# Sink logits from one bfloat16 product of three parts, and a shorter 1/sqrt, in a two-layer transformer kernel

## The chip, the core and the metric

The kernel runs on one core of one Trainium2 chip. The metric is the device time of one execution in microseconds. Differences are told in per cent of the time before, 2735.24 us.

## The reference, cut to what matters

The program is a trunk of two layers over 512 latent tokens and 256 context tokens with 1024 features. Each layer is a SwiGLU feed-forward, a mixer and a second feed-forward, every one behind an RMS norm with modulation. The mixer of layer 0 has two groups of heads, latent attention and window attention; that of layer 1 is gated linear attention. The window attention gives every query one more logit, the sink of its head, which takes part in the softmax and has no value:

```python
s_win = jnp.where(valid, s_win, NEG_INF)
s_ctx = jnp.einsum("bqngd,bknd->bngqk", qi, kc) * WIN_SCALE
pr = jax.nn.softmax(jnp.concatenate([s_ctx, s_win, sink_col], axis=-1), axis=-1)
```

The sink is one number for each of the 8 heads, the same for all queries. RMS norms stand in front of each sub-layer, on the queries and keys of both kinds of attention, on the latents, and on the outputs of the gated linear attention:

```python
rms_norm(t, g) = t / sqrt(mean(t * t) + 1e-6) * g
```

## The kernel before, in words

All large products are made of float32 data in three passes: a matrix is split into a high and a low part of type float32r (ScalarE copies the high part at L127, VectorE subtracts at L128), and TensorE multiplies high by high, high by low and low by high (L356 to L358, L368). TensorE takes its instructions in order; a weight load (PEld) and a product (PE) belong to each of them.

The layer-0 mixer is `pair_mixer`. Its first instructions (load of the norm gains at L722 and L724, the two scalings at L726 and L727, a bfloat16 identity at L729, the load of the sinks at L732, and the first weights) are issued while the last products of the feed-forward before it still run. The sinks lie in one row as [1, 8, 2] float32: the logit of each head, and beside it -1e30, so that a product has two columns.

Window attention runs in two calls of `win_attention`, one for each key/value head with its four query heads. `run_units` goes over 20 units in each: 4 units of context queries with two heads each, and 16 of latent queries with one head, which makes 24 score rows in a call and 48 in both. For one score row (`scores`, L1121 to L1137) TensorE multiplies the queries with the 256 context keys, with the window's keys, adds the band mask by a bfloat16 product with the identity (L1130; latent queries alone), and writes the sink into the two columns behind the scores:

```python
one = self.ones[0:1, :]
nc.tensor.matmul(out=s[:, n:n + 2], lhsT=one, rhs=sink[:, 4 * c + hd, :], start=True, stop=True)
```

The second line is L1137. Operands of plain float32 are multiplied in two passes, so it leaves two weight loads and two products in the trace. VectorE then takes the maximum of the row (L1065, tile nm), ScalarE the exponential (L1070), VectorE the reciprocal of the sum (L1032), GpSimd the scaling (L1035), TensorE transposes (L712), ScalarE and VectorE split the result (L1059, L1074), and TensorE multiplies with the values (L1158). Under it, in equal shares for every unit, other work of the mixer runs: in the first call the remaining input projections and the norm of the queries, in the second `latents`, with its keys, values and queries (tiles kn, va, qa), up to the norm of the first latent queries.

`rsqrt` (L130 to L144) gives 1/sqrt on small tiles, of 2 to 48 columns: a shift (L137) and a subtraction (L139) for a first guess, then three rounds of three operations (L142, L143, L144), all on VectorE, each needing the one before it. It is called 23 times: once at the start, in the norm ahead of the later sub-layers (tile rstd), eight times inside the layer-0 mixer (tile rs), and once for each of the 4 heads of the gated linear attention (tile gr).

The order of the instructions in each engine's queue is not that of the code alone. The program is built under `tile.TileContext(nc, schedule_with_timeline_sim=True)`: a planner follows its own estimate of all durations and, among the instructions that it takes to be ready, issues those first that stand earlier in the code or under `high_priority`.

Of the kernel before, what the change touches and what calls it, by code (L numbers as in the profile page):

```python
# [8 lines left out]
F32 = mybir.dt.float32  # L9
# [13 lines left out]
T = SEQ + CTX  # L23
# [4 lines left out]
ALL_SEGS = [(0, 256), (256, 512), (512, T)]  # context tokens, latent tokens  # L28
# [3 lines left out]
class Stage:  # L32
    """A sub-layer: loads its first weights, one unit after the other, then waits for its operand."""
# [14 lines left out]
class Net:  # L48
# [28 lines left out]
    # ---- the residual: four slots that hold other things inside a mixer, while it waits in DRAM --  # L77
# [25 lines left out]
    def load_split(self, src, n, pool=None, keep=4, slots=(None, None)):  # L103
        """n columns in two halves, each as (hi, lo)"""
        nc = self.nc
        res = []
        for j in range(2):
            raw = self.raw(src[:, j * (n // 2):(j + 1) * (n // 2)])
            p, bufs = (self.stage, 3) if pool is None else (pool, keep)
            if slots[j]:  # L110
                hi, lo = [self.x_slot(i, [128, n // 2], F32R) for i in slots[j]]
            else:
                hi = p.tile([128, 1024], F32R, tag="whi", name="whi", bufs=bufs)[:, :n // 2]
                lo = p.tile([128, 1024], F32R, tag="wlo", name="wlo", bufs=bufs)[:, :n // 2]
            self.split(raw, hi, lo)
            res.append((hi, lo))
        return res
# [7 lines left out]
    def split(self, src, hi, lo, e=None):  # L125
        """src (float32, SBUF) -> hi + lo, both float32r"""
# [4 lines left out]
    def rsqrt(self, out, v, shape):  # L131
        """out = 1/sqrt(v) for a small positive float32 tile"""
# [3 lines left out]
        t = self.small.tile(shape, F32, tag="rs_t", name="rs_t", bufs=1)  # L136
        nc.vector.tensor_scalar(out=i, in0=v.bitcast(I32), scalar1=1, scalar2=None,  # L137
# [3 lines left out]
        for _ in range(3):  # L141
            nc.vector.tensor_tensor(out=t, in0=out, in1=out, op=ALU.mult)  # L142
            nc.vector.scalar_tensor_tensor(out=f, in0=t, scalar=-0.5, in1=v, op0=ALU.mult, op1=ALU.mult)  # L143
            nc.vector.scalar_tensor_tensor(out=out, in0=f, scalar=1.5, in1=out, op0=ALU.add, op1=ALU.mult)  # L144

# [20 lines left out]
    def mod_finish(self, l, p):  # L166
        """bias; the scale piece becomes norm_g * (1 + scale), the FFN gates carry the 1/2"""
# [11 lines left out]
    def first_open(self, pool):  # L179
        """silu(c), silu(c_ctx) and zeros; the sum of four groups of 32 rows"""  # L180
# [14 lines left out]
    def first_product(self, pool, raw):  # L195
        """256 features of the vectors on the tensor engine, four products of 32 columns side by side"""
# [13 lines left out]
    def first_norm(self, pool, m, raw):  # L210
        """shift and scale of the first sub-layer, 128 features"""
# [7 lines left out]
    def first_gate(self, pool, i, raw):  # L219
        """half of the gate of the first sub-layer, 256 features"""  # L220
# [5 lines left out]
    def first_stats(self, pool):  # L226
        """1/rms of all tokens, on every partition"""
# [27 lines left out]
    def mod_queue(self, *pieces):  # L255
        """the products of the pieces (layer, number), in the two halves of the sums"""
# [6 lines left out]
    def mod_half(self, i):  # L263
        """a half of silu(c) and of silu(c_ctx) on every partition, for the background products"""
# [35 lines left out]
    def norm_squares(self, pool, seg, order=range(KT)):  # L300
        """sum over the features of a partition of the squares"""
# [13 lines left out]
    def norm_stats(self, seg, acc):  # L315
        """1/rms of each token of the segment, on every partition (PSUM)"""
# [36 lines left out]
    def mm3(self, out, w, x, first, last):  # L353
        """out += w^T x, w = (hi, lo) stationary, x = (hi, lo) moving"""
# [5 lines left out]
    def pair(self, w, nk, xk, segs, outs, cols=(0, 1)):  # L360
        """two column tiles of a weight unit, w[j] = (hi, lo) of [128, nk * 128], against the
        feature-major operand xk[k] = (hi, lo); outs[seg][j] are PSUM regions"""
# [9 lines left out]
    def regions(self, segs):  # L372
        """PSUM for two column tiles of each segment"""
# [22 lines left out]
    def close_out(self, load, nk, xk, segs, gate, nxt, off=0):  # L396
        """The last products of a sub-layer, in two passes over the weights: the norm of the first tokens runs
        under the products of the others, theirs under the first products of the next sub-layer, whose first
        weights come ahead of all that."""
# [46 lines left out]
    def ffn(self, l, sub, idx, segs, nxt, bg=(0, 0), first=4, start=False):  # L446
# [3 lines left out]
        # the first tiles: without the last segment, under the norm of it  # L450
# [9 lines left out]
        with st:  # L460
# [7 lines left out]
            def up(f, ss, regs=None):  # L468
                """the hidden tile f for the segments ss"""
# [13 lines left out]
            if start:  # L483
                # as the features come
# [61 lines left out]
    def seven_open(self, st, h, n0):  # L546
        """Gate and up columns (rows 1, 2) of a hidden tile against halves of the features and of the tokens,
        in seven products of halves in place of eight (Winograd's form of Strassen's)."""
# [50 lines left out]
        def start():  # L599
            """the place of the fourth block is free now"""  # L600
# [57 lines left out]
    def bcast(self, ap, n):  # L658
        """[128, a, b] -> [128, a, b, n] with a stride of zero"""
        return ap.unsqueeze(len(ap.shape)).to_broadcast(list(ap.shape) + [n])  # L660

    def rms_scale(self, pool, groups, shape, pool_squares=False):
        """1/rms of each group: groups = list of (ap [128, t, g, d], slice of the stats tile)"""
# [21 lines left out]
    def rope(self, pool, out, x, tab, nh, half):  # L685
        """x, out [128, nh, 2 * half] of one token tile; tab = (cos * gain, sin * gain) [128, 2 * half]"""
# [12 lines left out]
    def rot_tables(self, pool, nm, cos, sin, gain, d):  # L699
        """cos * gain and sin * gain, [128, 4, d]"""  # L700
# [14 lines left out]
    def pair_mixer(self, nxt, l=0):  # L715
        """Window attention of the first key/value head runs between the rest of the input projections,
        that of the second between the products of the latent attention's heads."""
        nc, tc, ins = self.nc, self.tc, self.ins
        with ExitStack() as es:
# [5 lines left out]
            # the score scales go with the query gains  # L725
# [5 lines left out]
            sink = ms.tile([1, 8, 2], F32, name="sink")  # L731
            nc.sync.dma_start(out=sink, in_=ins["sink_row"])  # L732
# [4 lines left out]
            z2 = wq[:, :, 4:8, :]  # window keys and values, until the second query chunk  # L737

            # window keys and the first queries: all but the last tokens under the norm of those
# [7 lines left out]
            def product(a, w, n, t, ks):  # L747
                """token tile t of a column chunk, token-major"""
# [56 lines left out]
            zk = self.x_slot(0, [128, 6, 192])  # latent keys, rotary keys, zeros  # L805
# [12 lines left out]
            oT = [None, None] + [self.x_slot(i, [128, 2, T]) for i in (2, 3)]  # MLA, window  # L818
# [8 lines left out]
            def background(gen, share):  # L827
                """a part of the work for each unit of attention; gen yields what it has spent"""
# [42 lines left out]
    def mixer_out(self, name, oT, segs, gate, nxt, oh=()):  # L871
        """oh: what is already in parts"""
# [12 lines left out]
    def norm_rope(self, pool, z, ng, parts):  # L885
        """the first ng groups of z [128, 6, .., 64] in place: RMS norm; then the gain and, for latent tokens, the
        rotation of each part (first group, last, gain, tables)"""
# [25 lines left out]
    def latents(self, lp, ml, zk, zq, gain, gcol, tabs, qa, kn, va, kr, kb):  # L913
        """MLA: normalised latents -> queries, keys, values, token-major"""
# [27 lines left out]
        def put(lat, w, out, sl, n):  # L942
            """token tiles of w^T lat for half of the columns"""
# [35 lines left out]
    def latent_queries(self, lp, gain, tabq, qa, t0):  # L979
        """norm and rotation of the MLA queries of two token tiles"""  # L980
# [15 lines left out]
    def rotary_keys(self, ml, kr, kb):  # L996
        nc = self.nc
        # rotary keys, shared by the heads: rows 64..95 of both key buffers
# [21 lines left out]
    def run_units(self, sp, units, score, probs, values, lanes):  # L1020
        """Attention, one unit after the other, every engine in this order: the scores of unit i, the
        transposition of the probabilities of unit i - 2, the products with the values that ended with
        unit i - 3; ahead of those, the other work of this iteration. A unit is one tile of queries of a
        head or two that see the context only; score(u) gives (PSUM scores, columns, key tiles) of each."""
# [53 lines left out]
    def win_attention(self, wp, c, wq, kT, vs, sink, identb, band, oT, bg):  # L1078
        """the four heads of key/value head c"""
        nc = self.nc  # L1080
        one = self.ones[0:1, :]
# [186 lines left out]
    def split_scaled(self, ps, col, hi, lo):  # L1268
        """PSUM * column -> hi + lo"""
# [6 lines left out]
    def gla_mixer(self, nxt, l=1):  # L1276
        """Both directions of a head run together, between the projections of the next head; the decays of
        the next head are ready before its keys and queries, which meet them on the way out of PSUM."""
# [8 lines left out]
        with ExitStack() as es:  # L1287
# [6 lines left out]
            # rows: high parts, low parts, high parts; those of the other factor: high, high, low  # L1294
# [524 lines left out]
```

## Time and profile before

| | |
|---|---|
| time, median of 3 runs | 2735.24 us (2733.0 to 2736.42) |
| span of the profiled execution, first to last instruction | 2731.1 us |
| TensorE products, busy | 2639.5 us (97%), 16848 instructions |
| TensorE weight loads, busy | 2450.8 us (90%), 16848 instructions |
| VectorE, busy | 2171.2 us (80%), 4540 instructions |
| ScalarE, busy | 1197.9 us (44%) |
| GpSimd, busy | 170.3 us (6%) |
| mean granted TensorE clock | 0.987 |

The profiled execution has no time of its own beside its span; the median of the runs is 4.1 us above that span. Times inside the execution are counted from its first instruction. [...]

### The profile page before, as it was taken

How to read it: one execution, taken by the hardware profiler on the slowest of the kernel's cores; microseconds unless marked ns; L12 is line 12 of the kernel's file. 1: busy time of each engine (PE TensorE's matmuls, PEld its weight loads, DVE VectorE, ACT ScalarE, POOL GpSimd, SP SyncE). 2: the span in 40 equal slices, each digit the busy share in tenths (PEclk: the TensorE clock that was granted, in tenths of full speed). 3: DMA queues.
4: the chain of work that ended last, by engine and by line, in shares of the span. 5: the costliest groups of instructions: out<-in, count | busy, mean ns of one | idle time of the engine just before them, and what ended most of it. 6: DMA issues, size and time to landing. Idle time of an engine off the chain costs nothing. (4 is left out here: it accounts for less than half of the span.)

```text
span 2731.1 us, 44146 instructions
## 1 busy us (share of the span) xinstructions
PE 2639.5 (97%) x16848; PEld 2450.8 (90%) x16848; DVE 2171.2 (80%) x4540; ACT 1197.9 (44%) x2254; POOL 170.3 (6%) x206
## 2 busy tenths in 40 slices
PE   7999999999978899999999999999999999899999
PEld 5899999989867789999999899999998999899899
DVE  5689798977788877797989877978777677778677
ACT  4324242445656753333324542424244555534444
POOL 0000000013344300000000000000000121000000
PEclk9999999999989999999999999999999999999999
DMA  8143444431000050433433314343233112422234
GB/s 311 41 144 119 137 132 143 132 126 31 24 24 1 1 170 24 126 120 122 130 124 110 126 47 144 100 149 105 91 105 102 55 63 70 147 64 97 96 108 130
DMA packets 103461, 279.30 MB, mean 102 GB/s; under 512 B 12146, under 2 KB 15090, under 8 KB 101714
## 3 DMA queue, kind: packets, MB, share of 16 engines
q1 hardware_dynamic: 103250, 276.49, 31.3%
q8 instruction: 132, 2.16, 0.3%
q14 instruction: 79, 0.65, 0.1%
HBM read 269.11 MB, written 7.34 MB: 101 GB/s over the span
## 5 line engine op out<-in xcount | busy, mean ns | idle before, releaser
L127 ACT ACTIVATE whi<-raw 128x512 fp32r<-128x512 f32 (+3 forms) x466 | 356.0, 767 | 730.7 <-PE r L368 324.2
L128 DVE TENSOR_TENSOR wlo<-raw,whi 128x512 fp32r<-128x512 f32 (+3 forms) x466 | 400.1, 861 | 72.3 <-ACT whi L127 69.7
L596 PE MATMUL r<-t,whi 128*128 128x384 f32 (+1 forms) x1704 | 401.2, 323 | 2.8 <-DVE u L633 2.0
L596 PE MATMUL r<-hh,wlo 128*128 128x384 f32 (+1 forms) x1136 | 366.3, 323 | 0.2
L596 PE MATMUL r<-hh,whi 128*128 128x384 f32 (+1 forms) x1136 | 365.8, 322 | 0.0
L596 PE MATMUL r<-hl,whi 128*128 128x384 f32 (+1 forms) x1136 | 365.8, 322 | 0.0
L291 DVE SCALAR_TENSOR_TENSOR junk<-wm,cb 128x512 bf16<-128x512 f32 x480 | 328.8, 685 | 13.1 <-ACT cb L270 8.0
L596 PEld LDWEIGHTS r<-t,whi 128*128 128x128 f32 x1704 | 295.6, 188 | 4.5 <-DVE u L633 2.8
L596 PE MATMUL r<-t,wlo 128*128 128x384 f32 (+1 forms) x852 | 273.3, 323 | 0.2 <-DVE wlo L128 0.2
L368 PE MATMUL r<-dh,whi 128*128 128x512 f32 (+1 forms) x952 | 267.3, 345 | 0.8 <-ACT whi L127 0.8
L368 PE MATMUL r<-dh,wlo 128*128 128x512 f32 (+1 forms) x952 | 266.8, 346 | 0.3 <-DVE wlo L128 0.3
L368 PE MATMUL r<-dl,whi 128*128 128x512 f32 (+1 forms) x952 | 266.8, 344 | 0.0
L127 ACT ACTIVATE whi<-s 128x512 fp32r<-128x512 f32 x284 | 174.9, 625 | 187.5 <-DVE s L618 75.2
L596 PEld LDWEIGHTS r<-hh,wlo 128*128 128x128 f32 x1136 | 213.4, 188 | 1.3 <-DVE wlo L128 1.3
L596 PEld LDWEIGHTS r<-hl,whi 128*128 128x128 f32 x1136 | 213.4, 188 | 0.8
L596 PEld LDWEIGHTS r<-hh,whi 128*128 128x128 f32 x1136 | 213.4, 188 | 0.3
L368 PEld LDWEIGHTS r<-dh,wlo 128*128 128x128 f32 x952 | 178.6, 188 | 24.3 <-DVE wlo L128 1.1
L368 PEld LDWEIGHTS r<-dh,whi 128*128 128x128 f32 x952 | 178.0, 188 | 24.5 <-ACT whi L127 2.7
L368 PEld LDWEIGHTS r<-dl,whi 128*128 128x128 f32 x952 | 178.1, 188 | 23.5
L128 DVE TENSOR_TENSOR wlo<-s,whi 128x512 fp32r<-128x512 f32 x284 | 190.6, 683 | 2.8 <-ACT whi L127 2.1
L392 DVE SCALAR_TENSOR_TENSOR x<-r,mod,x 128x512 f32<-128x512 f32 (+1 forms) x168 | 100.0, 631 | 87.3 <-PE r L368 86.9
L596 PEld LDWEIGHTS r<-t,wlo 128*128 128x128 f32 x852 | 159.9, 188 | 0.5 <-DVE wlo L128 0.5
(403 smaller groups left out, 5880.4 us busy)
## 6 DMA issues: line engine op xcount, KB each, us to landing
raw<-gu SPq DMA_DIRECT2D x176, 512.0 KB, 4.0
wm<-w_mod SPq DMA_DIRECT2D x240, 256.0 KB, 2.9
raw<-dn SPq DMA_DIRECT2D x88, 320.0 KB, 2.9
raw<-dn SPq DMA_DIRECT2D x64, 384.0 KB, 3.1
raw<-w_out SPq DMA_DIRECT2D x28, 512.0 KB, 3.7
m<-w_mod0a SPq DMA_DIRECT2D x12, 1024.0 KB, 10.2
raw<-w_in SPq DMA_DIRECT2D x8, 512.0 KB, 4.5
raw<-w_kq SPq DMA_DIRECT2D x8, 512.0 KB, 3.6
```

Source lines behind the costliest of these rows:

```text
L127: self.nc.scalar.activation(out=hi, in_=src, func=AF.Copy)
L128: (e or self.nc.vector).tensor_tensor(out=lo, in0=src, in1=hi.bitcast(F32), op=ALU.subtract)
L291: nc.vector.scalar_tensor_tensor(out=junk, in0=w, scalar=1.0, in1=self.cb[:, v, :], op0=ALU.mult, op1=ALU.mult, accum_out=self.acc[:, m, v ...
L368: nc.tensor.matmul(out=outs[s][j], lhsT=w[j][wi][:, k * 128:(k + 1) * 128], rhs=xk[k][xi][:, s0:s1], start=(k == 0 and i == 0), stop=(k == ...
L392: self.nc.vector.scalar_tensor_tensor(out=self.xs[m][:, s0:s1], in0=regs[s][j], scalar=gate[:, m, v:v + 1], in1=self.xs[m][:, s0:s1], op0= ...
L596: nc.tensor.matmul(out=o, lhsT=y[wi], rhs=x[k][xi], start=first and k == 0 and i == 0, stop=last and k == H - 1 and i == 2, skip_group_che ...
```

## The change

The sink logits are split once, ahead of the attention, into three bfloat16 parts that add up to the float32 number. The parts lie in rows 0, 32 and 64 of a [96, 8, 2] bfloat16 tile that is zero elsewhere, and one product with 96 rows of ones adds them. The ones are the upper halves of the float32 ones, read with a step of two elements. The loop over parts works in a pool that is closed again before the next tiles are made. In `rsqrt` the three rounds become one round of higher order with four operations and one with three, with other constants: 9 operations in place of 11. The rest of the diff takes comments and docstrings away.

```diff
-            sink = ms.tile([1, 8, 2], F32, name="sink")
-            nc.sync.dma_start(out=sink, in_=ins["sink_row"])
+            sink = ms.tile([96, 8, 2], BF16, name="sink")
+            nc.vector.memset(sink, 0.0)
+            sks = ExitStack()
+            sk = self.pool("sk", sks, side="right")
+            sink_f = sk.tile([96, 8, 2], F32, name="sink_f")
+            nc.sync.dma_start(out=sink_f, in_=ins["sink_row"].to_broadcast([96, 8, 2]))
+            sink_p = sk.tile([96, 8, 2], BF16, name="sink_p")
+            for r in (0, 32, 64):
+                nc.vector.tensor_copy(out=sink_p, in_=sink_f)
+                nc.vector.tensor_copy(out=sink[r:r + 1], in_=sink_p[r:r + 1])
+                if r < 64:
+                    nc.vector.tensor_tensor(out=sink_f, in0=sink_f, in1=sink_p, op=ALU.subtract)
+            sks.close()
...
-        one = self.ones[0:1, :]
+        one = self.ones.bitcast(BF16).rearrange("p (c two) -> p c two", two=2)[0:96, :, 1]
...
-        for _ in range(3):
-            nc.vector.tensor_tensor(out=t, in0=out, in1=out, op=ALU.mult)
-            nc.vector.scalar_tensor_tensor(out=f, in0=t, scalar=-0.5, in1=v, op0=ALU.mult, op1=ALU.mult)
-            nc.vector.scalar_tensor_tensor(out=out, in0=f, scalar=1.5, in1=out, op0=ALU.add, op1=ALU.mult)
+        nc.vector.tensor_tensor(out=t, in0=out, in1=out, op=ALU.mult)
+        nc.vector.tensor_tensor(out=f, in0=t, in1=v, op=ALU.mult)
+        stt(out=t, in0=f, scalar=-10.0 / 3.0, in1=f, op0=ALU.add, op1=ALU.mult)
+        stt(out=out, in0=t, scalar=5.0, in1=out, op0=ALU.add, op1=ALU.mult)
+        stt(out=t, in0=out, scalar=9.0 / 64.0, in1=out, op0=ALU.mult, op1=ALU.mult)
+        stt(out=f, in0=t, scalar=-3.0 / 16.0, in1=v, op0=ALU.mult, op1=ALU.mult)
+        stt(out=out, in0=f, scalar=9.0 / 16.0, in1=out, op0=ALU.add, op1=ALU.mult)
```

## Rows read from the trace of the kernel before

**Rows 1.** Stages of window attention: length, busy PE, PEld, DVE, ACT, POOL (count), clock.
```profile
640.50:656.00 15.50, 15.50 (x105) 14.30 (x104) 5.47 (x15) 8.94 (x25) 5.16 (x10) 0.89 0.01 1
656.00:723.00 67.00, 62.56 (x483) 57.85 (x481) 55.70 (x169) 40.14 (x99) 20.88 (x31) 0.97 0.12 35
723.00:735.00 12.00, 12.00 (x58) 9.99 (x56) 6.24 (x17) 7.51 (x22) 5.00 (x9) 0.72 0.00 0
735.00:759.00 24.00, 22.36 (x145) 18.58 (x143) 21.07 (x60) 19.15 (x46) 12.11 (x17) 1.00 0.06 24
759.00:777.50 18.50, 12.25 (x56) 9.60 (x57) 12.27 (x23) 7.92 (x16) 6.71 (x7) 0.72 0.08 28
777.50:806.50 29.00, 27.30 (x192) 25.18 (x190) 22.70 (x54) 20.76 (x49) 13.85 (x14) 1.00 0.02 2
806.50:836.00 29.50, 18.70 (x76) 14.65 (x76) 28.98 (x82) 9.95 (x25) 15.77 (x16) 0.60 0.11 36
```

**Rows 2.** Sink products, by tile: loads (minimum/median/maximum ns) and who waits.
```profile
L1137 PEld LDWEIGHTS s<-sink,ones x96: 181/184/333, 641.0 to 806.3; 1*128 1x128 f32 x96
...
  DVE nm L1065: 14.2, 14
```

**Rows 3.** Timeline of weight loads around one sink: start, duration, line.
```profile
658.20 0.10 PEld L1130 LDWEIGHTS <-identb 128*128 128x128 bf16 x1
658.36 0.29 PEld L1137 LDWEIGHTS s<-sink,ones 1*128 1x128 f32 x2
658.67 0.20 PEld L712 LDWEIGHTS t<-ident,pr 128*128 128x128 f32 x2
```

**Rows 4.** Timeline of weight loads around a band product with window keys behind it.
```profile
669.32 0.10 PEld L1130 LDWEIGHTS <-identb 128*128 128x128 bf16 x1
669.32 0.31 PEld L1126 LDWEIGHTS s<-wkT,wqT 128*128 128x128 f32 x2
```

**Rows 5.** Timeline in the latent attention: loads of 96 and of 128 rows.
```profile
839.45 0.28 PE L358 MATMUL s<-kb,q 96*128 96x256 f32 x1
839.47 0.25 PEld L712 LDWEIGHTS t<-ident,pr 128*128 128x128 f32 x2
...
845.55 0.38 PE L712 MATMUL t<-ident,qa 128*96 128x128 f32 x2
845.66 0.19 PEld L358 LDWEIGHTS s<-kb,q 96*128 96x128 f32 x1
```

**Rows 6.** An operation of 1/sqrt inside the layer-0 mixer, by tile (minimum/median/maximum ns).
```profile
L143 DVE SCALAR_TENSOR_TENSOR rs_f<-rs_t,ss x24: 157/191/1040, 614.4 to 826.9; 128x32 f32<-128x32 f32 x9, 128x36 f32<-128x36 f32 x3, 128x24 f32<-128x24 f32 x3, 128x12 f32<-128x12 f32 x3
```

**Rows 7.** Timeline at the norm of the latents: GpSimd and TensorE.
```profile
758.87 6.04 POOL L959 TENSOR_TENSOR kn<-kn,rs 128x512 f32<-128x512 f32 x6 [1.83 <-DVE rs_t L142]
...
765.78 1.79 PE L712 MATMUL t<-ident,x 128*128 128x128 f32 x6 [5.91 <-DVE x L965]
```

**Rows 8.** Timeline at the end of the gated linear attention.
```profile
2325.76 0.16 DVE L144 SCALAR_TENSOR_TENSOR gr<-rs_f,gr 128x4 f32<-128x4 f32 x1
2325.96 1.66 DVE L1649 SCALAR_TENSOR_TENSOR sg<-o,gr,sg 128x256 f32<-128x256 f32 x4
2326.50 1.97 PE L712 MATMUL c<-ident,sg 128*128 128x128 f32 x8 [4.56 <-DVE sg L1649]
```

**Rows 9.** Timeline where the mixer's first instructions stand, all engines.
```profile
526.03 0.42 SPq L724 DMA_DIRECT2D gcol<-gain_col  x1
...
526.50 0.33 SPq L732 DMA_DIRECT2D sink<-sink_row  x1
...
529.55 0.15 DVE L727 TENSOR_SCALAR gcol<-gcol 128x1 f32<-128x1 f32 x1 [0.84 <-DMA gcol<-gain_col]
529.62 0.95 DVE L128 TENSOR_TENSOR dl<-sg,dh 128x768 fp32r<-128x768 f32 x1
...
530.62 0.38 PE L368 MATMUL b<-dl,whi 128*128 128x256 f32 x1 [1.16 <-DVE dl L128]
```

**Rows 10.** Busy time and clock in the stretch behind that.
```profile
532.00:540.00 8.00, 8.00 (x57) 7.91 (x56) 6.64 (x17) 4.27 (x8) 0.00 (x0) 0.82 0.49 150
```

More of the change, by code (lines that the diff above doesn't have):

```diff
@@ L136, in rsqrt @@
         t = self.small.tile(shape, F32, tag="rs_t", name="rs_t", bufs=1)
+        stt = nc.vector.scalar_tensor_tensor
         nc.vector.tensor_scalar(out=i, in0=v.bitcast(I32), scalar1=1, scalar2=None,
```

## The prediction

> **What bounds the kernel now.** The busy times of the page come first: TensorE's products fill 97% of the span, so an edit pays where TensorE runs without a break and its own work gets shorter, or where it stands still for exactly the work that is cut. Both parts of the change lie mostly in the window attention of layer 0, so the next view is the table of stages [rows 1]. The reader is to see two kinds of stage in it. From 640.5 to 656 and from 723 to 735 TensorE is busy 15.50 us of 15.50 and 12.00 of 12.00, while VectorE is busy a third to a half and ScalarE about 60%: TensorE alone sets the pace. From 656 to 723, 735 to 759 and 777.5 to 806.5 it is busy 93 to 94%, but VectorE also 78 to 88%, so work taken from TensorE is soon stopped by VectorE. From 806.5 to 836 VectorE is busy 28.98 us of 29.50 and TensorE waits. [...]
>
> The third view is the sink tile [rows 2]: 96 loads, two for each of 48 score rows, and VectorE's maxima waited 14 times, 14.2 us in all, for the sink, because it ends each score row. The fourth is the timeline of loads [rows 3]. Behind the band's load at 658.20 the sink's first load comes 0.16 us later, and the next load only 0.31 us after that, at 658.67, though a sink product has two columns. Where a band product has window keys behind it, the next load starts in the same hundredth as its own, 669.32 [rows 4]. So the sink costs more than two short products: nothing is loaded ahead under it.
>
> **The sink product.** Removed for each score row are two loads and two products of one row; added are one load and one product of 96 rows in bfloat16. What that saves has two parts. The second pass goes in any case: the two loads together take 0.29 us [rows 3], one alone 0.184 [rows 2], so the second begins 0.11 us after the first. The rest is the loading ahead. Loads of 96 rows occur in the latent attention: one starts at 845.66, while products of 128 rows started at 845.55 still run, and a load of 128 rows starts at 839.47, 0.02 us after a product of 96 rows [rows 5]. A change between 96 and 128 rows thus keeps the loading ahead, a change to one row and back does not. If the new sink behaves like the band's bfloat16 load and product [rows 4], its load-to-load distance falls from 0.31 us to about 0.01, and a little of the 0.16 us ahead of it goes too; I take 0.05 of that. That makes 0.35 us for each sink, with 0.11 (the pass alone) and 0.47 (all of 0.31 + 0.16) as ends. A bfloat16 load of 96 rows with a step of two elements stands nowhere in the trace; the band's, with 128 rows and dense, is the nearest.
>
> [...] In the trace the one-row load waits, and loads of 96 and 128 rows run ahead [rows 3, 5]. [...]
>
> How much of 48 x 0.35 = 16.8 us reaches the end follows from the stages, which hold 8, 16, 8, 8 and 8 sinks (no sink from 759 to 777.5 and none behind 806.5). In 640.5 to 656 and 723 to 735 all of it: 8 x 0.35 = 2.8 us each. In 656 to 723, 735 to 759 and 777.5 to 806.5 I take half: 16 x 0.35 / 2 = 2.8, and 1.4 twice, since VectorE has 11.3, 2.9 and 6.3 us free there and its waits are in part for other engines. Sum: 2.8 + 2.8 + 2.8 + 1.4 + 1.4 = 11.2 us.
>
> **1/sqrt.** Each call loses two operations of VectorE. Each depends on the one before and starts 0.20 us behind it (2325.76 to 2325.96, [rows 8]), so 0.4 us a call, 23 calls. Where does TensorE wait for it? At the end of the gated linear attention it stands still for 4.56 us behind that chain [rows 8]: 0.4 us gained in full. At 765.78 it had waited 5.91 us for the norm of the latents [rows 7]. There operations of 1/sqrt on six columns took up to 1040 ns [rows 6], each beside one of GpSimd's six multiplications of 6.04 us in all. Two operations fewer would be worth 2 us if the long ones went; but GpSimd's six stay, as many operations will again be paired with them, and what goes are short ones: 0.4 us. In the VectorE-bound stretch from 797 on lie three calls, six operations of 0.19 us (median, [rows 6]): 1.1 us. Sum 1.9 us. The other 18 calls run under TensorE's products and I cost them at nothing; if their cover were gone, they would give 18 x 0.4 = 7.2 us more. A loss is excluded, since the kinds and sizes of operation remain and there are fewer.
>
> **The new preparation.** Nine operations of VectorE (a clear, six copies, two subtractions) and a load that VectorE must now wait for. Before, the sinks' load concerned only TensorE, over 100 us later. SyncE issues it at 526.50, 0.47 us behind that of gcol, which landed when VectorE went on at 529.55, after 0.84 us of waiting; behind that in VectorE's queue stood the split of dl, and TensorE waited 1.16 us for it [rows 9]. At the same 3.5 us the sinks land near 530.0. [...] Ends 0 and 3.6 us; I take 1.6.
>
> **Sum.** 11.2 + 1.9 - 1.6 = 11.5 us less. Against the profiled span that is 2731.1 to 2719.6 us; the median of the runs is 4.1 us above the span, so 2735.2 - 11.5 = 2723.7, rounded **2724 us**, 0.4% faster. About 0.2% (5.5 us) is what a measurement of this kernel tells from no change, so faster means below 2729.8.
>
> **Rivals.**
> 1. The loading ahead doesn't come: a change to 96 rows, the other type or the step of two still makes the next load wait, as it does behind the one-row product [rows 3]. Then 48 x 0.11 = 5.3 us are saved, two thirds of it (11.2 of 16.8, as above) on the path: 3.5 + 1.9 - 1.6 = 3.8 us, 2731 us. For it: no such load in the trace. Against it: [rows 4, 5].
> 2. VectorE takes over as the bound. If the three mixed stages give nothing, the two pure ones give 5.6 us: 5.6 + 1.9 - 1.6 = 5.9 us, 2729 us. For it: VectorE's 88% from 735 to 759 [rows 1]. Against it: the maxima waited 14.2 us for the sink itself [rows 2].
> [...]
>
> **How the numbers follow.** The forecast has 0.60, rival 1 0.17, rival 2 0.14, rival 3 0.09. The forecast's own range is 2714 to 2730. Its fast end: 0.47 us for each sink with the same shares is 15.0 us, no cost of preparation, some cover gone in the 18 calls (4 us): 15.0 + 1.9 + 4 = 21 us. Its slow end: 11.5 less the rest of the preparation's price (2 us) and half of the mixed stages' 5.6. The range of 8 in 10 reaches to rival 1 with its own 2 us: 2714 to 2733. Faster: 0.58 of the forecast, 0.05 of rival 1, 0.08 of rival 2, so 0.71. Same: 0.02 + 0.12 + 0.06 = 0.20. Slower: 0.09.
>
> **What would show it.** In the changed profile there is one load and one product for each of 48 sinks, and the load behind it starts within 0.05 us rather than 0.31; if it starts 0.1 to 0.2 us later, rival 1 holds. VectorE's wait for sinks falls below 14.2 us. The two pure stages shrink by about 2.8 us each; if they do and the mixed ones don't, rival 2 holds. TensorE's wait for the gate of the gated linear attention falls from 4.56 us to about 4.2. Near 530, the nine operations stand ahead of or behind dl, and TensorE's wait there says what they cost. [...]

## The result, and the profile after

The changed kernel takes 2716.22 us (median of 4 runs, 2714.96 to 2720.14) beside 2734.12 us (4 runs, 2730.45 to 2736.42) for the kernel before: a ratio of 0.9945, 95% interval 0.9930 to 0.9961. It is 17.9 us faster, where 11.5 were forecast. 2716 lies inside the range of 2714 to 2733, near its fast end.

The head of the page after, with the span and TensorE's line:

```profile
span 2715.1 us, 44020 instructions
...
PE 2617.5 (96%) x16800; PEld 2432.6 (90%) x16800; DVE 2162.7 (80%) x4503; ACT 1197.2 (44%) x2254; POOL 174.0 (6%) x206
```

TensorE has 48 loads and 48 products fewer and 22 us less of busy time; VectorE has 37 instructions fewer. The sink by tile, against [rows 2]:

```profile
L1155 PE MATMUL s<-sink,ones x48: 168/169/181, 640.1 to 789.9; 96*128 96x2 bf16 x48
...
  DVE nm L1083: 4.7, 4
```

VectorE's maxima now wait 4 times, 4.7 us, in place of 14 times, 14.2 us. The timeline of loads around one sink, in the same order of work as [rows 3], band, sink, next load:

```profile
653.15 0.10 PEld L1148 LDWEIGHTS <-identb 128*128 128x128 bf16 x1
653.16 0.10 PEld L1155 LDWEIGHTS <-ones 96*128 96x128 bf16 x1
653.22 0.31 PEld L718 LDWEIGHTS t<-ident,pr 128*128 128x128 f32 x3
```

From the band's load to the load behind the sink it is 0.07 us; before it was 658.67 - 658.20 = 0.47. The load behind stands 0.06 us after the sink's own, and within 0.002 us (median) of the start of the sink's product. The loading ahead came: the next load no longer starts 0.17 us behind the start of the last sink product (median before), but with it.

The stages answer to [rows 1], but cut at the same work, so that they can be compared: from the first sink to the 32nd, from there to the 40th, to the 48th, and from there to the 61st score product of the latent attention. Before (columns: length, busy PE, PEld, DVE, ACT, POOL with counts, then the granted clock):

```profile
640.95:732.98 92.03, 87.59 (x623) 79.96 (x623) 65.99 (x196) 55.05 (x141) 30.10 (x48) 0.93 0.09 25
732.98:756.94 23.96, 23.00 (x152) 19.57 (x151) 20.58 (x57) 19.64 (x47) 12.82 (x18) 1.00 0.06 24
756.94:806.17 49.23, 40.59 (x251) 35.36 (x249) 36.54 (x83) 29.27 (x65) 20.79 (x22) 0.90 0.03 11
806.17:859.44 53.27, 39.66 (x217) 32.21 (x215) 48.85 (x123) 28.59 (x71) 24.07 (x27) 0.78 0.07 21
```

After:

```profile
640.13:719.92 79.79, 71.43 (x593) 65.81 (x592) 63.03 (x191) 52.68 (x137) 28.48 (x46) 1.00 0.10 29
719.92:742.01 22.09, 20.93 (x145) 16.96 (x144) 19.50 (x51) 20.46 (x52) 15.00 (x20) 1.00 0.07 25
742.01:789.83 47.82, 36.53 (x244) 32.03 (x244) 37.13 (x85) 29.28 (x65) 20.23 (x22) 0.89 0.03 12
789.83:846.24 56.41, 39.95 (x216) 33.69 (x214) 47.34 (x118) 28.45 (x71) 25.37 (x28) 0.73 0.06 20
```

Two things stand out. The first stage became 12.2 us shorter, but its granted clock (1.00 or 0.50 throughout both traces, so a mean over the stage) also went from 0.93 to 1.00. And the last stage, where the forecast had a gain of 1.1 us for six VectorE operations fewer, became 3.1 us longer. Elsewhere TensorE's wait at the end of the gated linear attention fell from 4.56 to 4.17 us [rows 8]:

```profile
2309.82 1.97 PE L718 MATMUL c<-ident,sg 128*128 128x128 f32 x8 [4.17 <-DVE sg L1667]
```

And the wait for dl grew from 1.16 to 2.09 us [rows 9], because six of the eight operations that split the sinks stand ahead of dl (VectorE's timeline):

```profile
527.87 0.15 DVE L733 TENSOR_SCALAR gcol<-gcol 128x1 f32<-128x1 f32 x1 [0.86 <-DMA gcol<-gain_col]
528.06 0.17 DVE L746 CAST sink_p<-sink_f 96x16 bf16<-96x16 f32 x1
...
528.91 0.17 DVE L749 TENSOR_TENSOR sink_f<-sink_f,sink_p 96x16 f32<-96x16 f32 x1
529.01 0.95 DVE L128 TENSOR_TENSOR dl<-sg,dh 128x768 fp32r<-128x768 f32 x1
```

### The profile page after: what moved, and what is told of

Its sections match the earlier page's. It is cut to its first block, busy times and chain, and to the rows that moved or that the text cites. A ratio compares the mean times of both kernels' runs of the same rounds, so it can differ in the third digit from the quotient of the medians.

```text
span 2715.1 us, 44020 instructions
## 1 busy us (share of the span) xinstructions
PE 2617.5 (96%) x16800; PEld 2432.6 (90%) x16800; DVE 2162.7 (80%) x4503; ACT 1197.2 (44%) x2254; POOL 174.0 (6%) x206
```

## The experiments

**The two parts alone.** The first kernel is the changed one with the old 1/sqrt, the second the kernel before with the new one; of the first, cut at the dots:

```
-        nc.vector.tensor_tensor(out=t, in0=out, in1=out, op=ALU.mult)
-        nc.vector.tensor_tensor(out=f, in0=t, in1=v, op=ALU.mult)
...
-        stt(out=out, in0=f, scalar=9.0 / 16.0, in1=out, op0=ALU.add, op1=ALU.mult)
+        for _ in range(3):
+            nc.vector.tensor_tensor(out=t, in0=out, in1=out, op=ALU.mult)
...
```

For the second these lines go the other way round.

> The changed kernel with the 11 operations of 1/sqrt from before. Theory (the terms add up): the sink product carries nearly all of the 17.9 us, 15 to 17 us faster than before, a ratio of 0.9938 to 0.9945, and the one-off shifts near 125 and 2100 to 2200 us are not tied to it. Rival (the planner's new order made the gain, and the parts don't add): the two parts alone sum to something that differs from 17.9 us by more than 4 us.

Measured: 2725.38 us beside 2733.33, 8.0 us faster; ratio 0.9972 (0.9961 to 0.9982, which is 5 to 11 us).

> The kernel before with the 9 operations of 1/sqrt alone. Theory (the terms add up): 0.4 us at the end of the gated linear attention, about as much at the first norm, a little elsewhere: 1 to 2 us faster, ratio 0.9993 to 0.9996. Rival (order): 6 us or more in either direction, because every one of the planner's due times shifts.

Measured: 2718.44 us beside the same 2733.33, 14.9 us faster; ratio 0.9944 (0.9931 to 0.9956, 12 to 19 us); its slowest run, 2719.22, lies below the fastest of the kernel before, 2728.57. Nine operations in place of eleven, on tiles of 2 to 48 columns, bring nearly as much alone as the whole change. The theory fell on both: the sink carries half of what this expectation gave it, 1/sqrt some eight times as much, and 8.0 + 14.9 = 22.9 us is 5.0 more than the 17.9 of both together. Each of the three has an interval of 3 to 4 us to either side, so the times alone don't show that the parts fail to add. The profiles place the difference: the last stage took 53.51 us in the unchanged kernel's second execution (next section), 51.61 with 1/sqrt alone, 53.87 with the sink alone, and 56.41 with both.

How much of the sink's saving arrives, and where, is seen between 1/sqrt alone and both, which ran these stretches at the same clock: from the first sink to the 9th, to the 25th, and from the 41st to the 48th. With 1/sqrt alone:

```profile
638.18:653.99 15.81, 15.81 (x122) 14.63 (x121) 6.76 (x18) 10.38 (x27) 5.16 (x10) 1.00 0.00 1
653.99:716.03 62.04, 58.58 (x462) 54.09 (x461) 52.09 (x162) 38.35 (x97) 20.26 (x32) 1.00 0.12 37
...
767.02:794.88 27.86, 26.16 (x182) 24.18 (x182) 21.61 (x53) 20.00 (x47) 13.84 (x14) 1.00 0.00 1
```

With both:

```profile
640.13:653.22 13.09, 13.07 (x115) 12.52 (x114) 6.52 (x16) 10.05 (x27) 5.18 (x10) 1.00 0.01 1
653.22:714.47 61.25, 53.81 (x448) 49.47 (x447) 52.48 (x164) 37.77 (x97) 20.76 (x32) 1.00 0.13 38
...
763.57:789.83 26.26, 23.58 (x176) 22.01 (x176) 21.55 (x52) 20.05 (x48) 13.19 (x14) 1.00 0.00 1
```

The first stretch gives 2.7 us (forecast 2.8), the second 0.8 (2.8), the third 1.6 (1.4); the one between the 25th and the 40th sink gives 30.90 - 27.54 = 3.4 (4.2). From the 40th sink to the 41st, where no sink product stands, 20.09 us became 21.56: TensorE waits there for the norm of the latents, 5.0 us with 1/sqrt alone, 8.6 with the sink alone and 7.8 with both. With both, VectorE's queue has a split of weights between the last two operations of that norm's 1/sqrt (L149 and L150), and L150 starts only 2.06 us behind the split:

```profile
749.79 2.14 DVE L128 TENSOR_TENSOR wlo<-raw,whi 128x1024 fp32r<-128x1024 f32 x1
```

With 1/sqrt alone that split stands behind the norm. Whether this is all of the 1.5 us was not tried.

**What is scatter.** The two kernels unchanged, each profiled a second time.

> The kernel before, unchanged, a second profiled execution. [...]

Measured: 2732.37 us, ratio 1.0001 (0.9992 to 1.0011). The times agree and the traces don't: the second execution of the same program took from the first to the 32nd sink:

```profile
640.45:726.97 86.52, 81.77 (x623) 74.52 (x622) 65.34 (x196) 54.09 (x138) 29.21 (x46) 1.00 0.09 27
```

That is 5.5 us less than the first, with the clock at 1.00 in place of 0.93. The kernels of this study whose code in that stage is that of before (this one, and the two below with other calls altered) make four executions: 92.03 us at 0.93, 86.52 at 1.00, 90.56 at 0.94, 92.11 at 0.93. So the first profile's 12.2 us in that stage are 86.52 - 79.79 = 6.7 us of work and 5.5 of clock.

> The changed kernel, unchanged, beside the two with moved preparation. [...]

Measured: 2715.82 us beside 2732.80, ratio 0.9945 (0.9930 to 0.9960). First to 32nd sink again:

```profile
635.92:715.72 79.80, 71.45 (x593) 65.83 (x592) 63.00 (x191) 52.72 (x137) 28.48 (x46) 1.00 0.10 29
...
785.60:841.80 56.20, 40.28 (x217) 33.79 (x215) 47.32 (x118) 28.36 (x71) 25.38 (x28) 0.70 0.06 20
```

79.80 us beside 79.79, and the long last stage again, 56.20. So the length of both stages belongs to the kernel. Seven executions with a sink of 96 rows had that stage at 0.98 to 1.00. But 1/sqrt alone, with the old sinks, had 84.77 us at 1.00, and so had the unchanged kernel's second execution, so with the old sinks the clock is not always lower; why it often is was not tried.

**Rows or type.** One kernel has 96 rows in float32, two passes, no splitting; the other one row in bfloat16, one pass:

```
-            sink = ms.tile([1, 8, 2], F32, name="sink")
+            sink = ms.tile([96, 8, 2], F32, name="sink")
+            nc.vector.memset(sink, 0.0)
+            nc.sync.dma_start(out=sink[0:1], in_=ins["sink_row"])
...
-        one = self.ones[0:1, :]
+        one = self.ones[0:96, :]
```
```
-            sink = ms.tile([1, 8, 2], F32, name="sink")
+            sink_f = ms.tile([1, 8, 2], F32, name="sink_f")
+            sink = ms.tile([1, 8, 2], BF16, name="sink")
+            nc.vector.tensor_copy(out=sink, in_=sink_f)
...
-        one = self.ones[0:1, :]
+        one = self.ones.bitcast(BF16).rearrange("p (c two) -> p c two", two=2)[0:1, :, 1]
```

> The kernel before with one alteration: the sink's tile has 96 rows, row 0 the logits and the others zero, still float32 in two passes, and no splitting. Theory (the number of rows decides whether loads run ahead): the load behind a sink starts within 0.05 us of the second sink product instead of 0.17 us, each sink saves about 0.25 us of the 0.37 us, and with no preparation on VectorE the kernel is 10 to 13 us faster, about 2722 us. Rival (the type or the two passes decide): the load-to-load distance of 0.31 us stays and the time is that of before within 2 us.

> The kernel before with a sink of one row in bfloat16, one pass (it leaves out the two lower parts of the logits). Theory (the number of rows decides): the one-row load still waits for the band's product and the load behind it still waits for the sink's product, so only the second pass goes, 0.11 us for each of 48 sinks, 3 to 5 us of the whole: 2729 to 2731 us against 2734. Rival (the type decides): loads run ahead as in the changed kernel, 0.36 us for each sink, 2718 to 2720 us.

Measured: 96 rows in float32 2725.77 us, 7.6 us faster than before where 10 to 13 were expected, ratio 0.9966 (0.9952 to 0.9979); one row in bfloat16 2728.49 us, 4.3 us faster, ratio 0.9985 (0.9975 to 0.9995). The loads around one sink, with 96 rows in float32:

```profile
653.96 0.10 PEld L1131 LDWEIGHTS <-identb 128*128 128x128 bf16 x1
653.97 0.31 PEld L1138 LDWEIGHTS s<-sink,ones 96*128 96x128 f32 x2
654.12 0.51 PEld L712 LDWEIGHTS t<-ident,pr 128*128 128x128 f32 x4
```

With one row in bfloat16:

```profile
651.52 0.10 PEld L1132 LDWEIGHTS <-identb 128*128 128x128 bf16 x1
651.68 0.09 PEld L1139 LDWEIGHTS <-ones 1*128 1x128 bf16 x1
651.79 0.42 PEld L712 LDWEIGHTS t<-ident,pr 128*128 128x128 f32 x4
```

From the band's load to the load behind the sink: 0.47 us with one row and two passes [rows 3], 0.27 with one row and one pass, 0.16 with 96 rows and two passes (before a transposition, as here; 0.24 before the other products, and in the median), 0.07 with 96 rows and one pass. The sink's own load follows the band's by 0.16 us with one row of either type and by 0.01 with 96 rows of either type. So the number of rows decides the loading ahead, as forecast, and the type doesn't (one row and 96 were tried, none between); my expectation that the next load comes within 0.05 us of the second pass did not hold (median 0.08). By the products, from the band's to the one behind the sink, the medians of the 32 latent rows are 0.47, 0.27, 0.26 and 0.10 us. The second pass is worth 0.20 us with one row and 0.17 with 96, rather than 0.11.

**Which calls of 1/sqrt.** The kernel before, with the nine operations in some of the 23 calls:

```
-        for _ in range(3):
+        for _ in range(3 if not nine(self, nc, out, v, f, t) else 0):
...
+def nine(self, nc, out, v, f, t):
+    self.calls = getattr(self, "calls", 0) + 1
+    if not (self.calls in (1, 18, 19, 20, 21)):
+        return False
...
```

The seven new operations follow; the other two kernels name calls 4 to 11, and the ten that are left.

> The kernel before with the 9 operations in five of the 23 calls: the first, at 21 us, and the four of the gated linear attention, at 2176 to 2319 us. Theory (a shorter chain changes the queues' order around each call, and that is what pays): besides 0.4 us at each end, TensorE's waits of 1.05 us at 132 us and of 1.6 us at 2192 us, both behind other work, are gone; 4 to 5 us faster than before, and no shift between 140 and 2160 us. Rival (only the operations saved count): five times 0.4 us, 2 us at most, and both waits stay.

Measured: 2726.71 us beside 2730.86, 4.2 us faster; ratio 0.9984 (0.9975 to 0.9993).

> The kernel before with the 9 operations in the eight calls of layer 0's mixer alone (611 to 806 us). Theory (order around each call): 3 to 6 us faster, all of it between 630 and 840 us, TensorE's waits for VectorE's small tiles being fewer there; with the run of the other five calls that makes most of the 15 us of all 23. Rival (that stage's shift was scatter between executions): less than 1.5 us.

Measured: 2727.05 us beside the same, 3.8 us faster; ratio 0.9986 (0.9974 to 0.9998).

> The kernel before with the 9 operations in the ten calls that the two runs before left out, the norms between sub-layers (549 to 577, 979 to 1021, 1518 to 1543, 2035 to 2062 and 2347 to 2370 us). Theory (each call changes the order around it, and the effects add): 5 to 8 us faster, so that the three parts make the 15 us of all 23, and TensorE's wait of 0.83 us near 1612 us goes while those at 132 and 2192 us stay. Rival (the 15 us come of the parts together, or the trace places only half of them): less than 3 us, and the three parts fall 4 us or more short of 15.

Measured: 2730.86 us beside 2732.03, 1.2 us; ratio 0.9997 (0.9985 to 1.0009), no difference that can be told. What TensorE waits for near 132, 1612 and 2192 us tells the theories apart. The waits of the unchanged kernel's second execution:

```profile
PE r L596 <- DVE u L633: 1.0, 1, 1.0
...
PE r L596 <- ACT whi L127: 0.8, 1, 0.8
...
PE f L356 <- DVE gv L1449: 1.6, 1, 1.6
```

With the first call and the gated linear attention's four altered, the first and the third are gone and the second stays at 0.8. With calls 4 to 11 altered, all three stay. With the other ten altered, the second is gone, and 0.9 and 1.6 stay. So each wait hangs on one group of calls and not on the others. Not all are near: the only call of its group ahead of the wait near 132 us is the first, at 21 us, and the last ahead of the one near 1612 is at 1543. That it is the order of the queues, not the 0.4 us, is seen at the third; the other two were not followed. Before (VectorE, second execution of the unchanged kernel):

```profile
2186.98 0.90 DVE L128 TENSOR_TENSOR k<-B,k 128x512 fp32r<-128x512 f32 x1 [2.28 <-ACT k L127]
2187.79 3.65 DVE L128 TENSOR_TENSOR o<-x,o 128x512 fp32r<-128x512 f32 x2
2191.37 0.68 DVE L1449 TENSOR_TENSOR gv<-f,gv 128x512 fp32r<-128x512 f32 x1
...
2186.01 3.00 POOL L1524 TENSOR_TENSOR sg<-sg,gn 128x512 f32<-128x512 f32 x2 [13.14 <-ACT sg L1523]
2188.98 1.91 POOL L1518 TENSOR_TENSOR B<-B,col 128x768 f32<-128x768 f32 x1
```

With the nine operations everywhere:

```profile
2179.35 0.91 DVE L128 TENSOR_TENSOR o<-x,o 128x512 fp32r<-128x512 f32 x1 [1.84 <-ACT o L127]
2180.18 1.78 DVE L128 TENSOR_TENSOR k<-B,k 128x512 fp32r<-128x512 f32 x1
2181.89 0.68 DVE L128 TENSOR_TENSOR o<-x,o 128x512 fp32r<-128x512 f32 x1
2182.49 0.68 DVE L1455 TENSOR_TENSOR gv<-f,gv 128x512 fp32r<-128x512 f32 x1
...
2182.04 1.85 POOL L1524 TENSOR_TENSOR B<-B,col 128x768 f32<-128x768 f32 x1 [0.63 <-DVE k L128]
```

With the shorter chain the planner puts one o ahead of k. GpSimd's product on B waits for k (0.63 us in the second fence). With k first it runs beside the second o, as another of GpSimd's multiplications (on sg) does beside the first, and the two take 3.65 us; with o first it begins only when k is done, at 2182.04, and the last o, begun at 2181.89, takes 0.68. Company on GpSimd alone doesn't set these times: gv of the same size took 0.68 us in both fences, at 2191.37 behind B and at 2182.49 beside it. From the first of the three to gv it is 2182.49 - 2179.35 = 3.14 us in place of 2191.37 - 2186.98 = 4.39, and TensorE's wait of 1.6 us for gv is gone.

The three parts make 4.2 + 3.8 + 1.2 = 9.2 us of the 14.9. By the expectation's own mark, 4 us or more short, the rival holds for the sum; but each of the four intervals is 2.5 to 3.5 us wide to either side, so the 5.7 us may be scatter. The profiles show one candidate: from the first to the 32nd sink the kernel with calls 4 to 11 altered took 89.33 us at a clock of 0.94, the one with all 23 altered 84.77 at 1.00, 4.6 us less with the same sinks and the same calls in that stage. Whether the other calls bring that clock or the executions fell so isn't shown, since the unchanged kernel ran the stage at both.

**The stretch where both together lose.** The changed kernel with the preparation moved (below), and the old eleven operations in the last three calls of the mixer:

```
+        self.calls = getattr(self, "calls", 0) + 1
+        if self.calls in (9, 10, 11):
+            for _ in range(3):
+                nc.vector.tensor_tensor(out=t, in0=out, in1=out, op=ALU.mult)
...
+            return
```

> The changed kernel with the sinks' preparation moved, and with the old 11 operations in the last three of those eight calls, 780 to 806 us, where VectorE is nearly full. Theory (the 3 us that the changed kernel loses again from 790 to 810 us come of the order, since neither part alone loses them): with the longer chain back, that loss is under 1 us, and the kernel is 2 to 3 us faster than with 9 operations everywhere, 2711 us. Rival (VectorE's time decides there): six more operations of 0.19 us make it about 1 us slower, 2714 to 2715 us.

Measured: 2712.26 us beside 2730.86, ratio 0.9937 (0.9925 to 0.9950). Its last stage, against that of the changed kernel (56.41 us):

```profile
788.55:841.83 53.28, 38.98 (x216) 31.71 (x214) 48.49 (x124) 28.82 (x71) 24.86 (x28) 0.78 0.06 21
```

Six VectorE operations more, and the stage is 3.1 us shorter (with the preparation moved and nine operations everywhere it is 56.45 us), so VectorE's time does not decide there. The order does, as VectorE's timelines show for 2 of the 3 us. The changed kernel:

```profile
793.52 0.15 DVE L1050 RECIPROCAL rc<-sm 128x1 f32<-128x1 f32 x1
...
793.66 1.59 DVE L1006 TENSOR_TENSOR qa<-qa,rs 128x256 f32<-128x256 f32 x2
795.18 0.67 DVE L683 TENSOR_REDUCE ss<-tsq 128x8 f32<-128x512 f32 x1
795.77 0.57 DVE L1184 TENSOR_TENSOR x<-o,otmp 64x128 f32<-64x128 f32 x2
796.37 0.69 DVE L1083 TENSOR_REDUCE nm<-s 128x1 f32<-128x514 f32 x1
```

With the longer chain:

```profile
791.18 0.15 DVE L1054 RECIPROCAL rc<-sm 128x1 f32<-128x1 f32 x1
...
791.43 0.57 DVE L1188 TENSOR_TENSOR x<-o,otmp 64x128 f32<-64x128 f32 x2
792.03 0.69 DVE L1087 TENSOR_REDUCE nm<-s 128x1 f32<-128x514 f32 x1
```

The shorter chain makes rs ready sooner, and I read from this (the planner's own times are not on record) that it puts the scaling of qa (L1006) and a sum (L683) ahead of the output and the next score row's maximum: nm starts 2.85 us after the reciprocal in place of 0.85. In the time of the whole kernel the 3 us can't be told: 2712.26 us here and 2713.35 with nine operations everywhere, at ratios of 0.9937 and 0.9935.

**The preparation.** The split moved behind the first projections, to where the rotation tables are made; in a second kernel also the two scalings of gain and gcol:

```
-            sink_f = sk.tile([96, 8, 2], F32, name="sink_f")
-            nc.sync.dma_start(out=sink_f, in_=ins["sink_row"].to_broadcast([96, 8, 2]))
...
             nc.gpsimd.tensor_copy(out=band, in_=band_f)
+            sink_f = pp.tile([96, 8, 2], F32, name="sink_f")
+            nc.sync.dma_start(out=sink_f, in_=ins["sink_row"].to_broadcast([96, 8, 2]))
...
```

In the second kernel the tensor_scalar of gain and that of gcol follow the same line.

> The changed kernel with the sinks' load and the eight operations that split them moved behind the window attention's first projections, where TensorE has products queued. Theory (the six operations ahead of dl cost 0.95 us): TensorE's wait for dl falls from 2.1 to 1.2 us and the kernel is about 1 us faster than the changed one, 2715 us. Rival (the cost was hidden, or is paid again beside the rotation tables): within 0.5 us of the changed kernel, or slower.

Measured: 2713.35 us beside 2732.80, ratio 0.9935 (0.9921 to 0.9948), beside the changed kernel's 2715.82 on the same chip. The wait:

```profile
PE b L374 <- DVE dl L128: 1.0, 1, 1.0
```

It fell from 2.1 to 1.0 us. The medians differ by 2.5 us; of that, 1.1 is shown, and the rest is within the intervals.

> As the run with the preparation moved, and the two scalings that wait for gain and gcol (0.39 and 0.86 us of VectorE's time ahead of dl) moved there too. Theory: dl follows the gating product without a wait, TensorE's wait for dl goes or falls under 0.3 us, and the kernel is 2 to 3 us faster than the changed one, 2713 to 2714 us. Rival: something else is late next, the gating product sg itself or the last weights, and less than 1 us comes of it.

Measured: 2713.82 us, ratio 0.9936 (0.9921 to 0.9951). The scalings stood where they had been in VectorE's queue, right ahead of dl, and so did their waits (0.44 and 0.85 us). The wait for dl was 1.1 us. The move in the code was undone by the planner, so this tells nothing of what the waits cost.

## Why the prediction came out as it did

- **The sink product** was right in mechanism and in size: forecast 0.35 us for each, and the products stand 0.47 - 0.10 = 0.37 us closer. The share of it that arrives was too high: at an equal clock and with the same 1/sqrt, the five stages (the third and fourth taken together) give 2.7 + 0.8 + 3.4 + 1.6 = 8.5 us, where 11.2 were forecast. What is short above all is the stage from 656 to 723 with its 16 sinks, 0.8 in place of 2.8. That is the second rival's case in one of the three mixed stages, and in part: VectorE is busy 52.48 us of 61.25 there, but TensorE's waits are 3.4 us for VectorE and 3.6 for ScalarE. Alone the sink with its preparation is worth 8.0 us (5 to 11), where 11.2 - 1.6 = 9.6 were forecast.
- **The preparation** cost 0.93 us of TensorE's wait for dl (1.16 to 2.09); forecast 1.6 between 0 and 3.6. No run shows the 1.6 or its end of 3.6; what the runs showed in their place is this 0.93, and 1.1 us less of that wait with the preparation moved. The load that VectorE must wait for cost nothing: issued at 524.96, it had landed when VectorE came to it at 528.06, with no wait in the trace. Behind it the granted clock is the same before and after, a mean of 0.72 from 530 to 536 us and of 0.82 from 532 to 540 [rows 10].
- **1/sqrt** is the step that failed: "The other 18 calls run under TensorE's products and I cost them at nothing", and the whole term of 1.9 us. The direct part was right: 4.56 to 4.17 us at the end of the gated linear attention, and alone 5.9 to 5.0 us of waiting for the norm of the latents (forecast 0.4) and 53.51 to 51.61 us in the last stage (forecast 1.1). But alone the edit is worth 14.9 us. The runs showed in its place that three waits of 1.0, 0.8 and 1.6 us under other stages go with the calls whose chain is shortened, the third of them by a new order of the queues, and that the first 32 sinks went from 86.52 to 84.77 us. Between the second execution of the unchanged kernel and this one, 2728.4 - 2717.4 = 11.0 us of span, the waits near 132, 1612 and 2192 us make 3.3, the mixer's four stages 4.5 (212.77 to 208.31) and the end of the gated linear attention 0.4. The rest of the 14.9 stays open; the clock is a candidate. "A loss is excluded" was wrong as well: beside the new sink the shorter chain of the mixer's last three calls lengthened the last stage by 3 us.
- **A new order** was in the forecast only as a loss, with 0.09 (rival 3). It came as a loss between 742 and 846 us, 3.1 us in the last stage and 1.5 at the norm of the latents. At the wait near 2192 us it came as a gain. The total was near in part by luck: a gain too small in one term met a gain too large in the other and these losses.
- **The first rival** (no loading ahead) is out by the loads. Its price of 0.11 us for the second pass was too low: 0.20 with one row.
- **The range.** The slow end doesn't follow from its terms: 11.5 - 2 - 2.8 = 6.7 us is 2728.5, not 2730. The forecast doesn't hang on it.
- **Sum.** In the profiled executions the stages and waits named here give 6.7 + 1.9 + 1.4 (first three stages), - 3.1, - 0.9 (dl), + 0.4 (the end of the gated linear attention) + 0.4 (the first call, an estimate by its two operations) and 1.1 + 0.6 + 1.6 (the waits near 132, 1612 and 2192 us, of which 0.4 is left at the second) = 10.1 us, and the clock from the first to the 32nd sink 5.5: 15.6 of the 16.0 us between the spans. The four executions of the old stage average 90.3 us, so in the median run the clock is worth some 3.8 rather than 5.5. Some 4 us of the 17.9 are then not placed, about the interval's 4 us to either side.

## What to carry to other kernels

Where a planner orders the queues by its own times, price an edit of a small chain by the order around each of its places as well as by its operations: list TensorE's short waits behind each call, up to some 100 us behind, since here they went with two operations of 0.2 us. Run each part alone before crediting a sum, and profile the unchanged kernel twice before reading a shift of some microseconds as the edit's. The product of one row here stopped the loading ahead on both sides of it, 0.47 us from the band's product to the one behind the sink; padding it with zeros to 96 rows brought that to 0.26 in two passes and, in bfloat16, to 0.10 in one.

## What the runs showed of the hardware

- Behind a bfloat16 load of 128 rows, a one-row weight load starts 0.16 us later, one of 96 rows 0.01 us later, in bfloat16 and in float32 alike.
- VectorE's operations on two tensors of 128x512 took 0.68 us alone; beside multiplications on GpSimd one took 1.78 and two together 3.65, but another again 0.68. Which operation has the company depended on the order.
- The same instructions from the first to the 32nd sink took 86.5 to 92.1 us in four executions, with the granted clock at 1.00 to 0.93. That range is about half of the 8 to 13 us over which the runs of the unchanged kernel scatter.
